# Larger slots and coarser operations in an L2 pooling kernel: three 51.5 KB input slots, stores for two loads each, and small loads at the end

## The chip, the cores and the metric

The kernel runs on one core of a Trainium2 chip. The metric is the time of one execution on the device in microseconds; the median of nine runs stands for a kernel. VectorE is called DVE here and ScalarE ACT, as in the profile; SP is the engine whose queue issues most DMAs.

## The reference

The input x is 32 x 256 x 4096 float32 (134.2 MB), and p is 2. Every four neighbours in the last axis become one output, the root of the mean of their squares; the output is 32 x 256 x 1024 float32 (33.6 MB).

```python
for i in range(length // kernel_size):
    window = np.abs(x[:, :, i * kernel_size:(i + 1) * kernel_size]) ** p
    result[:, :, i] = np.mean(window, axis=-1) ** (1.0 / p)
```

Since windows never cross rows, the whole input can be taken as one flat array, cut into pieces whose length is a multiple of four, with the matching quarter of each piece as output.

## The kernel before

The flat input is 128 partitions times 262144 columns. It is cut into 32 loads of 8192 columns (`W`), 4 MiB each and 32 KB per partition. Four input tiles rotate (`in_pool`, `bufs=4`). The loads are collected into groups: seven groups of four, one of three and one of one. A group is a contiguous block of the input, in which a partition's part is contiguous too; each load takes a stretch of it (`x_block`, L65), and the group's output is stored by one DMA (`out_block`, L70).

The order is written by hand; each engine runs its own instructions in the order of the program, and the waits follow from the data. The SP queue issues the loads (L79): three ahead of the loop, and in round i of the loop load i + 3, which waits until the tile it overwrites has been summed. In round i the load's two halves of 4096 columns (`CH`) are taken in turn:

- ACT squares the half in place (L108).
- DVE sums each four squares into the group's output tile with a reduction (L112).
- ACT takes the root of the half before this one, with the factor 1/4 in its scale (L87), so that it need not wait for the sum of the half just squared. When that ends a group, ACT's queue issues the group's store (L91).

```python
held = {len(groups) - 1 - LAST - j for j in range(2)}
...
        if i == first + g - 1 and c + CH == W and group_of[i] not in held:
            nc.scalar.dma_start(out=out_block(group_of[i]), in_=ot)
...
    root(*pending)
    for gi in sorted(held):
        nc.sync.dma_start(out=out_block(gi), in_=ots[gi])
```

The stores of groups 6 and 7 are held back: they are issued on SP after all loads (L122), so that they lie in the DMA queue behind the last load. Two output tiles rotate among the groups and the last group has its own.

Of the kernel before, what the change touches and what calls it, by code (L numbers as in the profile page):

```python
# [1 line left out]

# [4 lines left out]


@with_exitstack
def kernel(  # L10
    ctx: ExitStack,
    tc: tile.TileContext,
    x: bass.AP,
    p: float,
    kernel_size: int,
    out: bass.AP,
):

    nc = tc.nc

    assert float(p) == 2.0, "kernel specialized for p == 2"
    k = int(kernel_size)
    assert k == 4, "kernel specialized for kernel_size == 4"  # L30

    P = nc.NUM_PARTITIONS
    fp32 = mybir.dt.float32
    xf = x.rearrange("b c l -> (b c l)")
    of = out.rearrange("b c l -> (b c l)")
    total = xf.shape[0] // P

    W = 8192
    CH = 4096
    GROUP = 4  # L40
    LAST = 1
    n = total // W
    assert n * W == total


    groups = []
    i = 0
    while i < n - LAST:
        g = min(GROUP, n - LAST - i)
        groups.append((i, g))  # L50
        i += g
    groups += [(j, 1) for j in range(n - LAST, n)]
    held = {len(groups) - 1 - LAST - j for j in range(2)}
    group_of = {}
    for gi, (first, g) in enumerate(groups):
        for j in range(g):
            group_of[first + j] = gi

    in_pool = ctx.enter_context(tc.tile_pool(name="in_pool", bufs=4))
    out_pool = ctx.enter_context(tc.tile_pool(name="out_pool", bufs=2))  # L60
    last_pool = ctx.enter_context(tc.tile_pool(name="last_pool", bufs=1))
    ctx.enter_context(tc.manual_schedule())


    def x_block(i):  # L65
        first, g = groups[group_of[i]]
        block = xf[first * W * P:(first + g) * W * P].rearrange("(p w) -> p w", p=P)
        return block[:, (i - first) * W:(i - first + 1) * W]

    def out_block(gi):  # L70
        first, g = groups[gi]
        return of[first * W * P // k:(first + g) * W * P // k].rearrange("(p w) -> p w", p=P)

    xts = {}
    ots = {}

    def load(i):
        xt = in_pool.tile([P, W], fp32)
        nc.sync.dma_start(out=xt, in_=x_block(i))  # L79
        xts[i] = xt  # L80

    def root(i, c):
        first, g = groups[group_of[i]]
        ot = ots[group_of[i]]
        at = ((i - first) * W + c) // k
        o = ot[:, at:at + CH // k]
        nc.scalar.activation(  # L87
            out=o, in_=o, func=mybir.ActivationFunctionType.Sqrt, scale=1.0 / k,
        )
        if i == first + g - 1 and c + CH == W and group_of[i] not in held:  # L90
            nc.scalar.dma_start(out=out_block(group_of[i]), in_=ot)  # L91

    for i in range(3):
        load(i)

    pending = None
    for i in range(n):
        if i + 3 < n:
            load(i + 3)
        gi = group_of[i]  # L100
        first, g = groups[gi]
        if i == first:
            pool = last_pool if i >= n - LAST else out_pool
            ot = pool.tile([P, g * W // k], fp32)
            ots[gi] = ot
        for c in range(0, W, CH):
            xh = xts[i][:, c:c + CH]
            nc.scalar.activation(  # L108
                out=xh, in_=xh, func=mybir.ActivationFunctionType.Square,
            )  # L110
            at = ((i - first) * W + c) // k
            nc.vector.tensor_reduce(  # L112
                out=ots[gi][:, at:at + CH // k],
                in_=xh.rearrange("p (n j) -> p n j", j=k),
                axis=mybir.AxisListType.X, op=mybir.AluOpType.add,
            )
            if pending is not None:
                root(*pending)
            pending = (i, c)
    root(*pending)  # L120
    for gi in sorted(held):
        nc.sync.dma_start(out=out_block(gi), in_=ots[gi])  # L122


# [1 line left out]
_INS = ['x', 'p', 'kernel_size']  # L126
_OUTS = [((32, 256, 1024), 'float32')]

_NUMBERS = {'p': 2.0, 'kernel_size': 4}


# [26 lines left out]
```

## Time and profile before

| | |
|---|---|
| median of 9 runs | 395.78 us (395.55 to 395.92) |
| the profiled execution, its own time | 395.87 us |
| its span in the trace | 393.7 us |
| ACT busy | 294.8 us (75%), 130 instructions |
| DVE busy | 282.8 us (72%), 64 instructions |
| HBM read and written | 134.22 MB and 33.55 MB, 426 GB/s over the span |
| DMA packets | 5906 (41 DMAs of 128 rows, 16 completion packets for each, 2 of the instruction queue) |
| load, issue to landing | 35.9 us median, 32 of them, 4096 KB each |

The span runs from the first instruction of the program to the last; the 2.2 us between it and the execution's time lie outside. A load's 35.9 us from issue to landing is mostly waiting in the queue: up to four are in flight. The part of the page on DMA queues divides the traffic in this way (columns: queue, packets, megabytes, and the time that the packets took as a share of sixteen DMA engines over the span):

```profile
q1 hardware_dynamic: 4896, 141.56, 83.9%
q10 hardware_dynamic: 1008, 26.21, 15.5%
q14 instruction: 2, 0.02, 0.0%
```

Queue q1 carries what SP issues: 32 loads and two stores. Queue q10 carries ACT's seven stores. The last one fetches instructions. The shares sum to over 99%.

### The profile page before, as it was taken

What the parts mean: (1) busy time and instruction counts of PE and PEld (TensorE: products, weight loads), DVE (VectorE), ACT (ScalarE), POOL (GpSimd) and SP (SyncE); (2) the same over time, 40 slices, a digit from 0 to 9 for tenths busy, and PEclk for the clock granted to TensorE, in tenths of its full rate; (3) what the DMA queues carried; (4) which work ended last, traced back from release to release, by engine and by line L of the source; (5) the groups of instructions that cost most, each with busy time, mean ns of one, the idle gap of its engine ahead of it and who ended that gap; (6) DMA issues with size and microseconds to landing.
All of it is one profiled execution on the core that took longest, in us unless ns stands there. A gap on an engine that the chain in (4) does not pass through costs nothing.

```text
span 393.7 us, 357 instructions
## 1 busy us (share of the span) xinstructions
DVE 282.8 (72%) x64; ACT 294.8 (75%) x130; POOL 0.2 (0%) x4
## 2 busy tenths in 40 slices
DVE  0399996729976399764988559866598846999992
ACT  1699987469883798828988189863998819999981
POOL 0000000000000000000000000000000000000000
DMA  8999999999999999999999999999999999999997
GB/s 346 453 426 426 426 426 383 436 449 433 430 426 426 426 443 430 450 430 433 426 426 426 436 433 443 437 430 430 426 426 436 436 436 440 430 433 426 426 435 314
DMA packets 5906, 167.79 MB, mean 426 GB/s; under 512 B 656, under 2 KB 656, under 8 KB 656
## 3 DMA queue, kind: packets, MB, share of 16 engines
q1 hardware_dynamic: 4896, 141.56, 83.9%
q10 hardware_dynamic: 1008, 26.21, 15.5%
q14 instruction: 2, 0.02, 0.0%
HBM read 134.22 MB, written 33.55 MB: 426 GB/s over the span
## 4 chain that ended last, share of the span: by engine, by line
DMA 72%; ACT 17%; DVE 9%; SPq 0%; issue 0%; ACTq 0%
DMA xt<-in_x_dram 72%; ACT xt L108 14%; DVE ot L112 9%; ACT ot L87 2%; SPq L79 0%; ACTq L108 0%
## 5 line engine op out<-in xcount | busy, mean ns | idle before, releaser
L112 DVE TENSOR_REDUCE ot<-xt 128x1024 f32<-128x4096 f32 x64 | 282.8, 4420 | 103.3 <-ACT xt L108 102.5
L108 ACT ACTIVATE xt<-xt 128x4096 f32<-128x4096 f32 x64 | 231.0, 3611 | 87.5 <-DMA xt<-in_x_dram 84.9
L87 ACT ACTIVATE ot<-ot 128x1024 f32<-128x1024 f32 x64 | 67.1, 1048 | 4.2 <-DVE ot L112 3.4
L108 ACT ACT_TABLE_LOAD x1 | 1.3, 1283 | 0.7 <-PEq L139 0.7
L87 ACT ACT_TABLE_LOAD x1 | 1.3, 1283 | 0.0
L139 POOL MEMSET const-bfloat16-1.0<- 128x1 bf16 x1 | 0.1, 103 | 0.0
L139 POOL MEMSET const-uint8-127<- 128x1 uint8 x1 | 0.1, 103 | 0.0
L139 POOL MEMSET const-float32-1.0<- 128x1 f32 x1 | 0.1, 100 | 0.0
L139 POOL MEMSET const-float32-0.0<- 128x1 f32 x1 | 0.1, 99 | 0.2 <-issue 0.2
## 6 DMA issues: line engine op xcount, KB each, us to landing
xt<-in_x_dram SPq DMA_DIRECT2D x32, 4096.0 KB, 35.9
out_dram<-ot ACTq DMA_DIRECT2D x6, 4096.0 KB, 23.6
out_dram<-ot SPq DMA_DIRECT2D x1, 4096.0 KB, 34.1
out_dram<-ot SPq DMA_DIRECT2D x1, 3072.0 KB, 12.3
out_dram<-ot ACTq DMA_DIRECT2D x1, 1024.0 KB, 5.6
```

The lines of the kernel that those rows point to most:

```text
L87: nc.scalar.activation(out=o, in_=o, func=mybir.ActivationFunctionType.Sqrt, scale=1.0 / k,)
L108: nc.scalar.activation(out=xh, in_=xh, func=mybir.ActivationFunctionType.Square,)
L112: nc.vector.tensor_reduce(out=ots[gi][:, at:at + CH // k], in_=xh.rearrange("p (n j) -> p n j", j=k), axis=mybir.AxisListType.X, op=mybir. ...
L139: nc = _bacc.Bacc("TRN2", target_bir_lowering=False, num_devices=1)
```

## The change

Three input tiles of 13184 columns (51.5 KB per partition) replace four of 8192, and two output tiles of 6592 columns (25.8 KB) replace the former ones. There are 22 loads instead of 32: loads 0 to 17 fill a slot each, loads 18 and 19 share a slot, and so do 20 and 21 (6592, 6592, 6592 and 5056 columns). Groups 0 to 8 have two loads each, group 9 has loads 18 to 20, and group 10 load 21. There are 11 stores instead of 9.

In loads 0 to 15 one square and one sum take the whole load. Loads 16 and 17 are taken in halves of 6592, load 21 in halves of 2528. One root of 6592 columns is taken per group in groups 0 to 8, and it stands on ACT behind the square of the following piece (`LAG`). At the end roots are finer: one for loads 18 and 19 together, one for load 20, and one for each half of load 21.

From load 17 on (`PAIRS`), the sum is made by two tensor additions in place of one reduction: neighbours are added in place at every second column, and then columns 0 and 2 of every four are added into the output.

The stores of groups 7 to 10 (`late`) are issued on SP, in order, after all loads. The outputs of groups 9 and 10 have no output tile: they lie in the third input tile, which load 17 was the last to use (`in_x`).

```diff
-    W = 8192
-    CH = 4096
-    GROUP = 4
-    LAST = 1
...
+    W, O_W = 13184, 6592
+    X_SLOTS, O_SLOTS = 3, 2
+    slots = [[(W, [W])]] * 16 + [[(W, [6592, 6592])]] * 2
+    slots += [[(6592, [6592]), (6592, [6592])], [(6592, [6592]), (5056, [2528, 2528])]]
+    groups = [2] * 9 + [3, 1]
+    late = {7, 8, 9, 10}
+    in_x = {9: (2, 0), 10: (2, 4944)}
+    FINE, ENDS, LAG = {21}, {19, 20}, 1
+    PAIRS = 17
...
+    def root(g, o, ends):
+        nc.scalar.activation(out=o, in_=o, func=Act.Sqrt, scale=1.0 / k)
+        if ends and g not in late:
+            store(g, nc.scalar)
...
+    def total_sum(o, v, i):
+        add = mybir.AluOpType.add
+        if i < PAIRS:
+            nc.vector.tensor_reduce(
+                out=o, in_=v.rearrange("p (n j) -> p n j", j=k),
+                axis=mybir.AxisListType.X, op=add,
+            )
+            return
+        h = v.rearrange("p (m t) -> p m t", t=2)
+        nc.vector.tensor_tensor(out=h[:, :, 0], in0=h[:, :, 0], in1=h[:, :, 1], op=add)
+        q = v.rearrange("p (n j) -> p n j", j=k)
+        nc.vector.tensor_tensor(out=o, in0=q[:, :, 0], in1=q[:, :, 2], op=add)
...
+        while ahead < n and loads[ahead][0] < s + X_SLOTS:
+            load(ahead)
+            ahead += 1
...
+        for step in chunks:
+            v = xs[i][:, c:c + step]
+            nc.scalar.activation(out=v, in_=v, func=Act.Square)
+            total_sum(ots[g][:, summed:summed + step // k], v, i)
+            while pending and pending[0][0] <= done - LAG:
+                root(*pending.pop(0)[1:])
...
+            ends = summed == columns[g] // k
+            if ends or i in FINE or (i in ENDS and c == w):
+                pending.append((done - 1, g, ots[g][:, rooted:summed], ends))
+                rooted = summed
+    for job in pending:
+        root(*job[1:])
+    for g in sorted(late):
+        store(g, nc.sync)
```

More of the change, by code (lines that the diff above doesn't have):

```diff
@@ L33 @@
     fp32 = mybir.dt.float32
+    Act = mybir.ActivationFunctionType
     xf = x.rearrange("b c l -> (b c l)")
@@ L36 @@
     total = xf.shape[0] // P
-    W = 8192
-    CH = 4096
-    GROUP = 4
-    LAST = 1
[L42 to L57, printed above, removed]
@@ L59 @@
-    in_pool = ctx.enter_context(tc.tile_pool(name="in_pool", bufs=4))
-    out_pool = ctx.enter_context(tc.tile_pool(name="out_pool", bufs=2))
-    last_pool = ctx.enter_context(tc.tile_pool(name="last_pool", bufs=1))
-    ctx.enter_context(tc.manual_schedule())
[L65 to L72, printed above, removed]
@@ L74 @@
-    xts = {}
-    ots = {}
[L77 to L91, printed above, removed]
@@ L93 @@
-    for i in range(3):
-        load(i)
-    pending = None
-    for i in range(n):
[L98 to L119, printed above, removed]
@@ L120 @@
-    root(*pending)
-    for gi in sorted(held):
-        nc.sync.dma_start(out=out_block(gi), in_=ots[gi])
+    W, O_W = 13184, 6592
[7 more added lines that the diff above has]
+    PAIRS = 17
+    loads = [(s, sum(w for w, _ in slot[:j]), *slot[j]) for s, slot in enumerate(slots)
+             for j in range(len(slot))]
@@ new lines @@
+    n = len(loads)
+    assert sum(w for _, _, w, _ in loads) == total
+    firsts = [sum(groups[:g]) for g in range(len(groups))]
+    assert sum(groups) == n
+    group_of = [g for g, count in enumerate(groups) for _ in range(count)]
+    columns = [sum(w for _, _, w, _ in loads[firsts[g]:firsts[g] + groups[g]])
+               for g in range(len(groups))]
+    x_pool = ctx.enter_context(tc.tile_pool(name="x_pool", bufs=1))
+    o_pool = ctx.enter_context(tc.tile_pool(name="o_pool", bufs=1))
@@ new lines, with block, load @@
+    x_tiles = [x_pool.tile([P, W], fp32, name=f"xt{j}") for j in range(X_SLOTS)]
+    o_tiles = [o_pool.tile([P, O_W], fp32, name=f"ot{j}") for j in range(O_SLOTS)]
+    ctx.enter_context(tc.manual_schedule())
+    def block(flat, g, div):
+        at, width = sum(columns[:g]) * P // div, columns[g] * P // div
+        return flat[at:at + width].rearrange("(p w) -> p w", p=P)
+    xs = {}
+    def load(i):
+        s, at, w, _ = loads[i]
+        v = x_tiles[s % X_SLOTS][:, at:at + w]
+        g = group_of[i]
+        src = sum(loads[j][2] for j in range(firsts[g], i))
+        nc.sync.dma_start(out=v, in_=block(xf, g, 1)[:, src:src + w])
+        xs[i] = v
@@ new lines, with store @@
+    ots = {}
+    def store(g, queue):
+        queue.dma_start(out=block(of, g, k), in_=ots[g])
+    def root(g, o, ends):
[14 more added lines that the diff above has]
+        nc.vector.tensor_tensor(out=o, in0=q[:, :, 0], in1=q[:, :, 2], op=add)
@@ new lines @@
+    ahead = 0
+    while ahead < n and loads[ahead][0] < X_SLOTS - 1:
+        load(ahead)
+        ahead += 1
+    pending = []
+    done = 0
+    for i in range(n):
+        s, _, w, chunks = loads[i]
+        while ahead < n and loads[ahead][0] < s + X_SLOTS:
+            load(ahead)
+            ahead += 1
+        g = group_of[i]
+        if i == firsts[g]:
+            t, first = (o_tiles[g % O_SLOTS], 0) if g not in in_x else (x_tiles[in_x[g][0]], in_x[g][1])
+            ots[g] = t[:, first:first + columns[g] // k]
+            summed = rooted = 0
+        assert sum(chunks) == w
+        c = 0
+        for step in chunks:
[4 more added lines that the diff above has]
+                root(*pending.pop(0)[1:])
+            done += 1
+            c += step
+            summed += step // k
+            ends = summed == columns[g] // k
+            if ends or i in FINE or (i in ENDS and c == w):
+                pending.append((done - 1, g, ots[g][:, rooted:summed], ends))
+                rooted = summed
```

## The prediction

> **What bounds the kernel now.** I read the page's slices first (part 2), because they show whether one resource is full all the way through.
>
> ```profile
> DVE  0399996729976399764988559866598846999992
> ACT  1699987469883798828988189863998819999981
> ...
> DMA  8999999999999999999999999999999999999997
> GB/s 346 453 426 426 426 426 383 436 449 433 430 426 426 426 443 430 450 430 433 426 426 426 436 433 443 437 430 430 426 426 436 436 436 440 430 433 426 426 435 314
> ```
>
> The 16 DMA engines are at nine tenths or more in every slice but the first and the last; DVE and ACT have holes everywhere. The table by stages says how full the middle is (columns: stretch, its length, busy time and count of DVE, ACT and POOL, clock, DMA share, GB/s):
>
> ```profile
> 60.00:350.00 290.00, 209.62 (x48) 216.77 (x97) 0.00 (x0) 1.00 1.00 432
> 350.00:380.00 30.00, 27.38 (x7) 28.25 (x13) 0.00 (x0) 1.00 1.00 433
> 380.00:390.00 10.00, 6.10 (x2) 3.79 (x3) 0.00 (x0) 1.00 0.97 407
> 390.00:394.00 4.00, 0.00 (x0) 0.00 (x0) 0.00 (x0) 1.00 0.40 170
> ```
>
> DMA share 1.00 at 432 GB/s up to 380 us. So only three things can change the time: DMA work itself, the dead time at both ends, and any hole that appears in the DMA stream. Next, the rows of part 5 give the prices:
>
> ```profile
> L112 DVE TENSOR_REDUCE ot<-xt 128x1024 f32<-128x4096 f32 x64 | 282.8, 4420 | 103.3 <-ACT xt L108 102.5
> L108 ACT ACTIVATE xt<-xt 128x4096 f32<-128x4096 f32 x64 | 231.0, 3611 | 87.5 <-DMA xt<-in_x_dram 84.9
> L87 ACT ACTIVATE ot<-ot 128x1024 f32<-128x1024 f32 x64 | 67.1, 1048 | 4.2 <-DVE ot L112 3.4
> ```
>
> The two ACT rows give 0.834 ns a column and 194 ns fixed. Last, the end of the timeline shows why there is no hole now: the held stores are issued while earlier transfers still run.
>
> ```profile
> 373.61 3.62 ACT L108 ACTIVATE xt<-xt 128x4096 f32<-128x4096 f32 x1 [0.55 <-DMA xt<-in_x_dram]
> ...
> 378.20 0.34 SPq L122 DMA_DIRECT2D out_dram<-ot  x1
> ...
> 387.25 0.34 ACTq L91 DMA_DIRECT2D out_dram<-ot  x1
> ```
>
> The last load lands at 373.5. The store of group 6 (4 MiB, 9.7 us) covers 373 to 382, group 7's (issued at 378.2) covers 382 to 390, and the last, issued at 387.25, follows without a gap.
>
> [...]
>
> **DMA work.** The bytes stay. Before, 32 loads and 9 stores have 128 rows each, 8 per engine: 328 packets an engine. After, 22 loads and 11 stores: 264. The trace's packet records have 32 KB in 1213 ns, 24 KB in 912, 8 KB in 309: 36.8 ns per KB and 8 ns over, of which 4 overlap the next packet. 64 x 4 ns = 0.3 us gained. Bounds 0 and 0.6 (no overlap).
>
> **Instruction fetches.** Part 3 of the page has two packets on the instruction queue; they stand at 159.7 and 250.8 us in the packet records, and the DMA engine beside them finishes at 392.5, the other fifteen between 391.5 and 392.0. As the built programs list them, ACT's instructions shrink from 137 to 47 and DVE's from 66 to 34, so I take these fetches as gone: 0.5 us, bounds 0 and 0.6. The start (first packet at 1.74 us) and the slow first store (its neighbours took about 1.2 us longer at 58 us) stay: first load and first ACT-queue store are there as before, counted at nothing.
>
> **Steady part.** A square of 13184 columns is 0.19 + 13184 x 0.834 ns = 11.2 us, a sum 13.9 (14.2 if all 4420 ns scale), a root of 6592 is 5.7. Loads land 9.71 us apart for 4 MiB when alone (22.47, 32.18, 41.90), so a 13184-column load takes 15.6 us, 23.4 beside a store of 7.8. Per two loads ACT has 28.1 us and DVE 27.8 against 39.0 of DMA: no bound. Refill of three slots, at its tightest: load 0 lands at about 18.8, is squared at 30.0 and summed at 43.9, so load 3's packets start at 44.9 (1 us from issue to first packet, as at 0.73 to 1.74), while loads 0 to 2 keep the queue full until 48.5. Slot 1 is 3.6 us early likewise (60.5 against 64.1). From load 4 on, a store widens this. The new wait of a sum for the store two groups before it is met about 6 us early (root and issue 18 us after a load's landing, 23.4 for the transfer, against 51 us); behind it only DVE's next sums queue. The sums that the SP loads wait for are the same waits as now, with longer sums. Cost 0; a lost cover would cost 1 us per us of lateness, not more.
>
> **The end.** Here the cover is thin. Stores 7 to 10 (three groups and the last load) go out on SP behind all loads, in order (before, two on SP and the last on ACT's queue); store 9 needs the root of load 20, and store 10 is queued behind its wait; nothing else is. Count from T, the landing of load 16. DMA still has load 17 (15.6), loads 18 to 20 (7.8 each), load 21 (6.0), stores 7 and 8 (7.8 each) and about 1 us of store 6: it runs dry at T - 0.4 + 61.6 = T+61.2. Without a penalty the engines go: ACT squares 16a, roots group 7, squares 16b, 17a, 17b, 18 (5.6 us each: 5.69 less 0.09 overlap) until T+33.7. DVE sums 16a by reduce (7.0) to 12.8, 16b, which waits for its square, from 16.9 to 24.0. Then come pairs of additions: 3296 outputs[...] and 1648 (1.87 us), 5.46 a pair. 17a and 17b end at 34.9, root of group 8 at 40.6, squares 19 and 20 at 46.2 and 51.8, sum 19 at 51.7, the joint root of 18 and 19 (2.9) at 54.7, square 21a at 56.9, sum 20 at 57.2, its root (1.6) at 58.8: store 9's first packet at T+59.8, 1.4 us early. So with the plain price nothing is lost.
>
> But the second addition reads every fourth fp32, a step of 16 bytes[...]. The first steps 8 bytes[...] and is priced plainly. For the second I bound the price from 1 cycle an element (1.87 us[...]) to 2 cycles[...]. I take 2, an estimate[...]. A pair is then 7.2 us. 17a and 17b end at 38.4; root of group 8 at 44.1; pair 18 at 45.6; squares 19, 20 at 49.7, 55.3; pair 19 at 56.9; the joint root at 59.8; square 21a 62.0; pair 20 at 64.1; its root 65.7; first packet 66.7. DMA stands still from 61.2 to 66.7: 5.5 us. Store 9 (5.9 us) then lasts to 72.6, and store 10, ready at about 71.6 + 1, follows. A further 0.1 us for each of the two to three dependent pairs on this path makes it 5.7.
>
> **Sum.** The profiled execution took 395.87 us (span 393.7 and 2.2 around it), 0.09 over the median. 395.87 - 0.3 - 0.5 + 5.7 = 400.8; against the median, 400.7.
>
> **Rivals.** *The second addition costs its plain price* (chance 0.41). [...] Then store 9 is in time and 395.78 - 0.8 = 395.0, or 395.1 with a little of the 1.4 us margin lost; not slower. It decides at about 1.25 cycles an element, where the margin is used up. [...]second addition 2.73 us, pair 6.3; the path grows by four times 0.86, 3.4, less the margin of 1.4, and the same 0.1: +2.1, 397.1 (0.12). *A refill hole*: slots 0 or 1 come free over 3.6 us late, because sums of 13184 take more than the 14.2 us above; each us late is added once or twice, 396 to 398 with the plain price (0.03). That the change does nothing at all is excluded: the instructions do differ.
>
> **Numbers.** Forecast (2 cycles) 400.7, own range 399.8 to 402.2, chance 0.44. A measurement of this kernel tells about 0.2% (0.8 us) from no change. Slower: 0.44 + 0.12 + 0.01 of the refill case = 0.57. The plain-price case, centred at 395.1, splits near 395.0: 0.18 faster and 0.23 same, to which the refill case adds 0.02: 0.25. Range: from 394.7 to 401.6, leaving out about 0.08 below and 0.1 above.
>
> **What would show it.** Right: additions of 1648 outputs near 3.6 us, DMA share near zero for 5 to 6 us just before the last two stores, the last but one store issued after its predecessor has landed. Packets about 4750 (33 x 144), fewer instruction fetches. Wrong: 1.87 us for that row and an unbroken DMA line; or a DMA dip near 48 or 64 us, which would be the refill.

## The result, and the profile after

The changed kernel takes 398.07 us (median, 397.31 to 398.54); the kernel before, over all its runs beside it, 395.70 us. The ratio is 1.0058 (95% interval 1.005 to 1.0067): slower by 2.4 us. The forecast was 400.7 us, slower by 5.0. The profiled execution took 398.41 us with a span of 396.4, against 395.87 and 393.7.

First the slices of the changed kernel's page (tenths of a slice, 9.9 us each):

```profile
DVE  0009898695959296929691969296919697699594
ACT  1095699929880998199619962996299639997973
...
DMA  8999999999999999999999999998999999999967
GB/s 341 426 458 442 431 436 436 359 434 474 397 466 436 426 426 418 426 434 436 458 452 426 391 455 428 428 468 386 434 436 439 476 426 426 394 436 428 435 287 321
```

The DMA row stands at nine tenths, with a single 8, up to the last slice but one, where it drops to 6 and 287 GB/s; before, it fell only in the last. The table by stages puts a place to it (stretch, its length, busy time and count of DVE, ACT, POOL, clock, DMA share, GB/s):

```profile
60.00:300.00 240.00, 170.29 (x13) 174.46 (x21) 0.00 (x0) 1.00 1.00 432
...
350.00:380.00 30.00, 25.22 (x9) 25.77 (x6) 0.00 (x0) 1.00 1.00 428
380.00:383.00 3.00, 2.97 (x2) 3.00 (x2) 0.00 (x0) 1.00 0.98 422
383.00:385.00 2.00, 2.00 (x2) 0.67 (x1) 0.00 (x0) 1.00 0.16 66
385.00:388.00 3.00, 2.78 (x3) 2.88 (x2) 0.00 (x0) 1.00 0.25 105
388.00:392.00 4.00, 2.75 (x2) 1.77 (x3) 0.00 (x0) 1.00 0.93 396
```

From 60 to 300 us the DMA is as full, at the same 432 GB/s, as before. Between 383 and 388 us it nearly stands still, while DVE has no idle time in the first two of these microseconds and 0.2 us in the next three: now DVE is what is waited for. The chain that ended last shows this less well than it seems to: DMA has fallen from 72% of the span to 47%, and DVE has risen from 9% to 22%. But 14 of these 22 are the reductions (L93), nearly all of them in the stretch where the DMA is full, and the first experiment below, which has no hole, shows 47% and 19%. So the hole is read from the table by stages and from the timeline, not from these shares (before; the change, by engine and by line; the first experiment):

```profile
DMA 72%; ACT 17%; DVE 9%; SPq 0%; issue 0%; ACTq 0%
...
DMA 47%; ACT 24%; DVE 22%; issue 6%; SPq 0%; ACTq 0%
DMA xt<-in_x_dram 47%; ACT xt L123 18%; DVE ot L93 14%; ACT ot L86 6%; DVE xt L99 4%; DVE xt L101 2%; DVE ot L101 2%; ACT xt L86 1%; ACT L86 0%; SPq L77 0%; ACTq L83 0%
...
DMA 47%; ACT 26%; DVE 19%; issue 6%; SPq 0%; ACTq 0%
```

What DVE does there, and at what price, is in the groups kept apart by shape (line, engine, operation, output and input, count, busy us, mean ns of one, idle before):

```profile
L93 DVE TENSOR_REDUCE ot<-xt 128x3296 f32<-128x13184 f32 x16 | 222.2, 13886 | 105.2 <-ACT xt L123 105.2
L123 ACT ACTIVATE xt<-xt 128x13184 f32<-128x13184 f32 x16 | 179.1, 11191 | 91.9 <-DMA xt<-in_x_dram 90.2 <-ACT ot L86 1.7
L86 ACT ACTIVATE ot<-ot 128x6592 f32<-128x6592 f32 x9 | 51.2, 5685 | 2.9 <-DVE ot L101 2.9
...
L99 DVE TENSOR_TENSOR xt<-xt 128x3296 f32<-128x3296 f32 x5 | 18.0, 3595 | 4.6 <-ACT xt L123 4.6
...
L101 DVE TENSOR_TENSOR xt<-xt 128x1648 f32<-128x1648 f32 x3 | 9.4, 3148 | 0.1
```

L101 is the second addition. It has half as many outputs as the first (L99), and yet takes 3.15 us against 3.60: 1.7 times the 1.87 us that the prediction calls its plain price. The trace of before has no addition, so the forecast's prices were its author's estimates: 3.59 us for a first one of 3296 outputs (3.60 here) and 1.87 to 3.59 for a second one; the 1.87 is measured below. The end of the timeline shows where that lands (start, us, engine, line, in brackets the idle time before it and what ended it):

```profile
323.07 5.70 ACT L123 ACTIVATE xt<-xt 128x6592 f32<-128x6592 f32 x1 [9.56 <-DMA xt<-in_x_dram]
...
360.34 5.70 ACT L86 ACTIVATE ot<-ot 128x6592 f32<-128x6592 f32 x1 [2.93 <-DVE ot L101]
...
381.96 3.13 DVE L101 TENSOR_TENSOR xt<-xt 128x1648 f32<-128x1648 f32 x1
...
385.12 1.58 ACT L86 ACTIVATE xt<-xt 128x1648 f32<-128x1648 f32 x1 [1.45 <-DVE xt L101]
...
386.73 6.12 SPq L83 DMA_DIRECT2D out_dram<-xt  x2
```

T is 323.07: taken here and below as the start of load 16's square, some 0.4 us after the load has landed. The root of group 8 and the root of load 20 both wait for a second addition, and store 9 goes out at 386.73, T+63.7. The packet records hold, for each DMA, sixteen completion packets (528 for 33 DMAs), taken here as one from each DMA engine; in what follows "the middle one" is the median of the sixteen and "the latest one" the last, and a hole is the time from there to the next DMA's first packets. Store 8 ends at 383.4 us on the middle one of the sixteen DMA engines and at 385.2 on the latest; store 9's first packets stand at 387.6. The hole is 4.3 us on most engines, and 2.4 on the latest one. The latest one sets the end: the span before and its hole make 393.7 + 2.4 = 396.1, against the span of 396.4.

### The profile page after: what moved, and what is told of

Read it like the earlier page. It is cut to its first block, busy times and chain, and to the rows that moved or that the text cites. A ratio compares the mean times of both kernels' runs of the same rounds, so it can differ in the third digit from the quotient of the medians.

```text
span 396.4 us, 192 instructions
## 1 busy us (share of the span) xinstructions
DVE 274.9 (69%) x32; ACT 281.7 (71%) x40; POOL 0.2 (0%) x4
## 2 busy tenths in 40 slices
DMA packets 4752, 167.77 MB, mean 423 GB/s; under 512 B 528, under 2 KB 528, under 8 KB 656
## 4 chain that ended last, share of the span: by engine, by line
DMA 47%; ACT 24%; DVE 22%; issue 6%; SPq 0%; ACTq 0%
DMA xt<-in_x_dram 47%; ACT xt L123 18%; DVE ot L93 14%; ACT ot L86 6%; DVE xt L99 4%; DVE xt L101 2%; DVE ot L101 2%; ACT xt L86 1%; ACT L86 0%; SPq L77 0%; ACTq L83 0%
## 5 line engine op out<-in xcount | busy, mean ns | idle before, releaser
L93 DVE TENSOR_REDUCE ot<-xt 128x3296 f32<-128x13184 f32 (+1 forms) x18 | 236.2, 13123 | 110.8 <-ACT xt L123 108.9
L123 ACT ACTIVATE xt<-xt 128x13184 f32<-128x13184 f32 (+2 forms) x25 | 223.2, 8938 | 102.1 <-DMA xt<-in_x_dram 100.4
L86 ACT ACTIVATE ot<-ot 128x6592 f32<-128x6592 f32 x9 | 51.2, 5685 | 2.9 <-DVE ot L101 2.9
L99 DVE TENSOR_TENSOR xt<-xt 128x3296 f32<-128x3296 f32 (+1 forms) x7 | 20.9, 2991 | 5.8 <-ACT xt L123 5.8
L101 DVE TENSOR_TENSOR xt<-xt 128x1648 f32<-128x1648 f32 (+1 forms) x5 | 12.0, 2404 | 0.2
L86 ACT ACTIVATE xt<-xt 128x632 f32<-128x632 f32 (+2 forms) x4 | 6.0, 1493 | 5.0 <-DVE xt L101 5.0
L101 DVE TENSOR_TENSOR ot<-xt 128x1648 f32<-128x1648 f32 x2 | 6.2, 3125 | 0.1
```

The costliest lines, as they stand in the source:

```text
L86: nc.scalar.activation(out=o, in_=o, func=Act.Sqrt, scale=1.0 / k)
L93: nc.vector.tensor_reduce(out=o, in_=v.rearrange("p (n j) -> p n j", j=k), axis=mybir.AxisListType.X, op=add,)
L99: nc.vector.tensor_tensor(out=h[:, :, 0], in0=h[:, :, 0], in1=h[:, :, 1], op=add)
L101: nc.vector.tensor_tensor(out=o, in0=q[:, :, 0], in1=q[:, :, 2], op=add)
L123: nc.scalar.activation(out=v, in_=v, func=Act.Square)
```

## The experiments

The theory is that the price of the second addition, whose inputs step 16 bytes, makes store 9 late. The rivals are other parts of the change: the coarse operations, the store layout, the transfers themselves. Beside each run the kernel before was timed on the same chip; it took 395.6 to 395.8 us there. What is read from packet records is always that of one profiled execution.

**The second addition reads every second column.** The first addition writes its sums side by side, so that the second steps 8 bytes; the number of outputs is the same.

```diff
-        nc.vector.tensor_tensor(out=h[:, :, 0], in0=h[:, :, 0], in1=h[:, :, 1], op=add)
-        q = v.rearrange("p (n j) -> p n j", j=k)
-        nc.vector.tensor_tensor(out=o, in0=q[:, :, 0], in1=q[:, :, 2], op=add)
+        m = v.shape[1] // 2
+        nc.vector.tensor_tensor(out=v[:, :m], in0=h[:, :, 0], in1=h[:, :, 1], op=add)
+        q = v[:, :m].rearrange("p (n j) -> p n j", j=2)
+        nc.vector.tensor_tensor(out=o, in0=q[:, :, 0], in1=q[:, :, 1], op=add)
```

> The first addition of a pair writes its results side by side, so that the second reads every second column (8 bytes apart) instead of columns 0 and 2 of four (16 bytes apart); nothing else changes. Theory (the 16-byte step makes the second addition slow, and DVE's queue is what store 9 waits for): the second addition of 1648 outputs falls from 3.13 us to about 1.87, a pair from 6.73 to 5.46, store 9 is issued about 5 us earlier relative to the landing of load 16, before store 8 has left the queue; the hole of 2.4 us on the latest DMA engine goes, and the time is 395.4 to 395.8, a ratio of 0.999 to 1.000. Rival (the small loads and ACT's own work at the end make the hole): still 397 to 398. Rival (the larger slots make the steady part slower): still above 397 with no hole at the end.

Measured: 395.71 us, ratio 1.0004 (0.9995 to 1.0012). Its group of second additions, its table by stages and the issue of store 9:

```profile
L102 DVE TENSOR_TENSOR xt<-xt 128x1648 f32<-128x1648 f32 x3 | 5.6, 1874 | 0.1
```

```profile
380.00:383.00 3.00, 1.92 (x2) 3.00 (x2) 0.00 (x0) 1.00 0.98 422
383.00:386.00 3.00, 2.29 (x2) 1.23 (x3) 0.00 (x0) 1.00 0.99 426
```

```profile
381.36 5.66 SPq L83 DMA_DIRECT2D out_dram<-xt  x2
```

The addition takes 1.87 us, the plain price of the prediction, store 9 goes out at T+58.8 (T is 322.53), the very time that the prediction worked out for the plain price, and the hole is gone. One access pattern is worth the whole 2.4 us.

**The duration alone, put back.** To the kernel above, two additions in a scratch tile are added between the two additions of each pair of loads 17 to 20. Their results are not used; they add only to DVE's time.

```diff
+    scratch = o_pool.tile([P, 450], fp32, name="scratch")
+    nc.vector.memset(scratch, 0.0)
...
+        if m > 2000:
+            for _ in range(2):
+                nc.vector.tensor_tensor(out=scratch, in0=scratch, in1=scratch, op=add)
```

> The kernel with the 8-byte step, and between the two additions of each pair of loads 17 to 20 DVE also adds a scratch tile of 450 columns to itself twice (2 x 0.63 us, results unused), which puts back the 1.25 us by which the 16-byte step was slower. Theory (the time comes from DVE's duration alone): the hole before store 9 is back, 2 to 2.5 us on the latest DMA engine, and the time is that of the changed kernel, 397.7 to 398.4. Rival (the 16-byte step did harm in another way, or the layout of the sums matters): about 395.7.

Measured: 397.47 us, ratio 1.0052 (1.0038 to 1.0065). The two groups:

```profile
L105 DVE TENSOR_TENSOR scratch<-scratch 128x450 f32<-128x450 f32 x10 | 6.2, 624 | 0.2
L107 DVE TENSOR_TENSOR xt<-xt 128x1648 f32<-128x1648 f32 x3 | 5.6, 1869 | 0.0
```

The loss comes back with time that touches none of the kernel's data: store 9 goes out at 385.66, T+62.9, and the hole on the latest engine is about 1.7 us. The median is 0.2 us under the expected range, since operations overlap a little (a second addition starts at 375.67 us, 0.08 before the two in the scratch tile end): from start to start, a pair on the path is 1.03 us longer here than in the first experiment, and 1.21 longer in the change. Over four pairs that is 0.7 us, by which store 9 goes out sooner than in the change. So it is DVE's duration that counts, not something else that the access pattern might do.

**One reduction in place of the additions.** `PAIRS = 99` in place of 17.

> The sums of loads 17 to 21 are made by one reduction each, as for the other loads, in place of two additions. Theory: a reduction of 6592 columns takes 7.02 us against 6.73 for the pair; four of them lie on the path to store 9, so the hole grows by about 1.2 us, and the time is 399.0 to 399.5 (ratio 1.009). So the pair as written saves only 1 us or so of the 6 us that a pair at the plain price would save (4 times 7.02 - 5.46). Rival (ACT sets the end): no change, 398.

Measured: 399.31 us, ratio 1.0092 (1.0078 to 1.0106), inside the expectation. Store 9 goes out at T+64.7, and the hole on the latest engine is 3.4 us, 1.0 longer than in the change:

```profile
383.00:386.00 3.00, 3.00 (x1) 1.35 (x1) 0.00 (x0) 1.00 0.08 35
```

A reduction of 6592 columns takes 7.0 us, a pair 6.7. The pairs of the change are thus a little better than what they replace, but only with the closer step (5.5 us) are they fast enough.

**Store 9 in two parts.** Loads 18 and 19 are stored apart from load 20.

```diff
-        store(g, nc.sync)
+        if g == 9:
+            cut = 3296
+            nc.sync.dma_start(out=block(of, g, k)[:, :cut], in_=ots[g][:, :cut])
+            nc.sync.dma_start(out=block(of, g, k)[:, cut:], in_=ots[g][:, cut:])
+        else:
+            store(g, nc.sync)
```

> The store of group 9 is cut in two: the outputs of loads 18 and 19 go out as soon as their joint root is done, those of load 20 after its own root; sums as in the changed kernel (16-byte step). Theory (DVE's chain sets when the last results exist, not how they are stored): the hole before store 9 closes, since its first part is issued 5 us earlier, but a hole of about 2.4 us opens before store 10, whose results still come 69.4 us after the landing of load 16; no gain, 397.8 to 398.3. Rival (the fault is that store 9 is one large piece waiting for its last part): the 2.4 us are won, 395.7.

Measured: 398.07 us, ratio 1.0063 (1.005 to 1.0076), as slow as the change. The issues, and the stage in which the hole now lies:

```profile
381.22 0.33 SPq L139 DMA_DIRECT2D out_dram<-xt  x1
386.45 0.33 SPq L140 DMA_DIRECT2D out_dram<-xt  x1
392.23 0.33 SPq L83 DMA_DIRECT2D out_dram<-xt  x1
```

```profile
390.00:392.00 2.00, 1.40 (x2) 0.53 (x1) 0.00 (x0) 1.00 0.05 20
```

The hole moves behind the split parts, in front of store 10: what is late is the end of the work of ACT and DVE, whatever is stored in between.

**Coarse operations undone, in loads 0 to 15.** `[[(W, [W])]] * 16` becomes `[[(W, [6592, 6592])]] * 16`: halves, as before the change.

> Loads 0 to 15 are squared and summed in halves of 6592 again (one root per store stays). Theory (the loss lies in the tail alone; the steady part has 3.6 us and more of cover at each refill): no change beyond 0.5 us, 397.6 to 398.5. Rival (coarse operations delay refills or stores in the middle): 0.5 to 2 us faster.

Measured: 399.00 us, ratio 1.0084 (1.007 to 1.0098): not as expected, 0.9 us slower than the change. Store 9 is issued at T+63.6 as in the change, but T is 323.96, 0.9 later. Two instruction fetches stood at 295.3 and 351.1 us, so two explanations were left: the fetches (theory B), or that finer operations issue store 6 sooner, so that its packets pass ahead of load 16's last ones (theory A). The next run tells them apart.

**Halves in loads 12 to 15 alone**, with the rest as in the change.

> Only loads 12 to 15 are taken in halves. Taking all of 0 to 15 in halves cost 0.9 us where I had expected nothing. Theory A: with halves the root of group 6 comes after half a square, so that store 6 starts some 5.6 us earlier and gets ahead of load 16; load 16 lands 0.9 us later and less of store 6 is left as cover after it: then these four loads do all of it, 399.0, and load 16 lands near 324.0 us. Theory B: the longer program fetches instructions in mid-run (at 295 and 351 us) and one DMA engine falls behind: then, with fewer added instructions and no fetch before load 16, 398.1.

Measured: 400.46 us, ratio 1.012 (1.0106 to 1.0134). No fetch stood ahead of the end, and yet it is slower still, so theory B doesn't account for it. T is 325.11, 2.0 us later than in the change, and store 9 follows at T+63.6 again:

```profile
388.75 6.12 SPq L83 DMA_DIRECT2D out_dram<-xt  x2
```

In the packet records, store 6 lands 6.0 us after load 16 in the change (328.7 and 322.7), 0.6 us ahead of it with halves everywhere (322.9 and 323.5), and 0.1 ahead of it here (324.6 and 324.7). Its last packets then no longer lie behind T, and the latest engine runs dry at T+60.2 in both runs, against T+62.1 in the change. That is theory A in kind: store 6 is issued at 296.13 us with halves everywhere and at 297.50 here, at 301.93 in the change, and both runs lose the same 1.9 us of cover. That the loss comes out as 0.9 us in the one run and 2.4 in the other, 1.5 more than expected, goes with how late the latest DMA engine is: it ends store 8 at 384.2 us with halves everywhere (0.7 behind the middle one), at 385.2 in the change (1.8 behind) and at 385.3 here (2.1 behind). Why it differs from run to run wasn't found.

**The price by itself.** A kernel that only times operations on tiles: three of each, 1648 outputs, with one thing changed at a time. A few of its lines:

```python
        nc.vector.tensor_tensor(**tt(flat, at(xt, 2), at(yt, 2)))
        nc.vector.tensor_tensor(**tt(flat, at(xt, 3), at(yt, 3)))
        nc.vector.tensor_tensor(**tt(flat, at(xt, 4), at(yt, 4)))
        nc.vector.tensor_tensor(**tt(at(ot, 4), x1, y1))
```

> No pooling at all: three tiles are loaded and fp32 additions of 1648 outputs run one after the other on DVE with various steps of their inputs and outputs, then squares on ACT; the output is one tile. Theory (the step of 16 bytes on the reading side is the cost): inputs with steps of 1 and 2 columns take 1.87 us, of 4 about 3.1, of 8 about the same; with one of the two inputs at step 4 also near 3.1; the pattern of the kernel (columns 0 and 2 of the same tile) 3.1. Rival (it is two readings of the same line from both inputs that collide): separate tiles at step 4 take 1.87 and only the pattern of the kernel 3.1. Rival (a step of the output or in-place writing costs): additions with a stepped output are slower and those with stepped inputs are not.

Measured (L60, L62, L64, L66 are additions with both inputs at steps 2, 3, 4 and 8; L74 has step 4 on the output alone; L81, L83, L85 are ACT squares with steps 1, 2 and 4):

```profile
L85 ACT ACTIVATE ot<-yt 128x1648 f32<-128x1648 f32 x3 | 9.4, 3144 | 0.1
L66 DVE TENSOR_TENSOR ot<-xt,yt 128x1648 f32<-128x1648 f32 x3 | 9.3, 3113 | 0.1
L74 DVE TENSOR_TENSOR ot<-xt,yt 128x1648 f32<-128x1648 f32 x3 | 9.2, 3079 | 0.1
...
L64 DVE TENSOR_TENSOR ot<-xt,yt 128x1648 f32<-128x1648 f32 x3 | 9.2, 3075 | 0.1
...
L62 DVE TENSOR_TENSOR ot<-xt,yt 128x1648 f32<-128x1648 f32 x3 | 7.1, 2364 | 0.1
...
L60 DVE TENSOR_TENSOR ot<-xt,yt 128x1648 f32<-128x1648 f32 x3 | 5.6, 1875 | 0.1
L83 ACT ACTIVATE ot<-yt 128x1648 f32<-128x1648 f32 x3 | 5.3, 1770 | 0.1
L81 ACT ACTIVATE ot<-yt 128x1648 f32<-128x1648 f32 x3 | 4.7, 1577 | 0.1
```

The cost is flat up to step 2 (1875 ns), rises at step 3 (2364), is full at step 4 (3075) and hardly higher at 8 (3113). It is the same with one input (3078 ns), both (3075), or the output at step 4 (3079), and with the kernel's own pattern, columns 0 and 2 of one tile (3072); so it is neither two inputs meeting in one line, since separate tiles pay it too, nor the output alone. DVE's fixed time follows from two plain additions: 3595 ns for 3296 outputs (L99) and 1875 for 1648 make 1.04 ns an element and 155 ns over. Without these, step 4 costs (3075 - 155)/1648 = 1.77 ns an element, step 3 (2364 - 155)/1648 = 1.34, three quarters of it. These prices suggest a count: with a tile divided into lines of 16 bytes, a division of the author's that no trace shows, four elements at step 3 touch three lines, at step 4 four lines, at step 2 only two.

**Does the count of lines give every pattern?** If so, a cost of about 1.78 ns for each line touched (at step 4 above, DVE 1.77 and ACT 1.79), with the engine's own rate as the least, should do so.

```python
        nc.vector.tensor_tensor(**tt(flat, at(xt, 5), at(yt, 5)))
        nc.vector.tensor_tensor(**tt(out2, rows(xt, 8, 2), rows(yt, 8, 2)))
        nc.vector.tensor_tensor(**tt(at(ot, 4), at(xt, 4), at(yt, 4)))
        nc.scalar.activation(out=sq, in_=at(yt, 3), func=Act.Square)
```

> No pooling: loads three tiles, then fp32 additions of 1648 outputs and squares with other steps; one tile is stored. Theory ([...]an element costs the larger of the engine's own rate and its share of lines): additions at step 5 and 7 take 3.07 to 3.12 us as at 4; at step 3 2.36; pairs of neighbours out of every four (two elements a line) 1.88; pairs out of every eight also 1.88; inputs and output all at step 4 3.1, not double; squares on ACT at step 3 near 2.4 us, at step 5 3.14, with the output at step 4 3.14. Rival (the cost grows with the distance, or adds up over operands): steps 5 and 7 above 3.2, and all three at step 4 well above 3.1.

Measured (L72 has all three operands at step 4; L64 is step 5; L70 takes two neighbours out of every eight; L75 is ACT at step 3):

```profile
L64 DVE TENSOR_TENSOR ot<-xt,yt 128x1648 f32<-128x1648 f32 x3 | 9.5, 3157 | 0.1
L72 DVE TENSOR_TENSOR ot<-xt,yt 128x1648 f32<-128x1648 f32 x3 | 9.4, 3147 | 0.1
...
L75 ACT ACTIVATE ot<-yt 128x1648 f32<-128x1648 f32 x3 | 7.3, 2418 | 0.1
...
L70 DVE TENSOR_TENSOR ot<-xt,yt 128x1648 f32<-128x1648 f32 x3 | 5.6, 1875 | 0.1
```

Two neighbours out of eight step 32 bytes from pair to pair and still cost the plain price (1875 ns), as the count of two elements to a line has it. Three strided operands cost hardly more than one (3147 ns against 3078). A price by the size of the step is refuted (3113 ns at step 8, 3075 at step 4); one by lines touched fits all patterns within 3%, but for ACT at step 2 (1770 ns; half a line an element gives 200 + 1648 x 0.89 = 1667). The 200 ns are ACT's fixed time, 1577 - 1648 x 0.834 with the prediction's price of a column. That the price goes by lines is a rule that fits the durations, not something seen in a trace.

**The gain that didn't come.** Without the hole the change should be 0.8 us faster than before, by the prediction's first two steps; the first experiment is not (395.71). In its packet records the middle DMA engine ends at 390.8 us, before at 391.7: 1.0 earlier. But the latest one ends at 392.2, 1.4 behind the middle one; before, 392.5, 0.7 behind. (The thirteen executions of the first experiment lie between 394.93 and 396.42 us, so the lag may well change from one to the next.) Two runs look for the lag's cause, both on top of the first experiment's edit. The one puts the steady stores on SP's queue:

```diff
-            store(g, nc.scalar)
+            store(g, nc.sync)
```

> The kernel with the 8-byte step, and the stores of groups 0 to 6 issued on SP's queue, where they stand between the loads, in place of ACT's. The 8-byte kernel gained nothing on the kernel before though its middle DMA engine ends 1 us earlier, because the latest engine lags the middle one by 1.4 us (0.9 in the kernel before). Theory (engines drift apart where packets of 51 KB and 26 KB from two queues alternate): with one queue the lag shrinks to below 1 us, and the time to 394.9 to 395.3. Rival (the lag comes from the start and from stalls that strike a few engines whatever the queue): 395.5 to 396.

Measured: 397.13 us, ratio 1.004 (1.0026 to 1.0054): refuted. The spread between the first and the last DMA engine grows from 1.3 us to 1.9, 2.4, 2.7 and 3.1 as stores start, and the latest engine ends at 393.7, the middle one at 391.1. Two queues are not the cause of the lag; with one it is larger.

The other cuts each full load in two DMAs of 25.8 KB per partition:

```diff
+        if w == W:
+            cut = w // 2
+            nc.sync.dma_start(out=v[:, :cut], in_=block(xf, g, 1)[:, src:src + cut])
+            nc.sync.dma_start(out=v[:, cut:], in_=block(xf, g, 1)[:, src + cut:src + w])
+        else:
+            nc.sync.dma_start(out=v, in_=block(xf, g, 1)[:, src:src + w])
```

> The kernel with the 8-byte step, and each load of 13184 columns made of two DMAs of 6592. Theory (drift comes from large packets): the lag between engines shrinks, 395.2 to 395.5 in spite of 144 more packets per engine at 4 ns each (0.6 us). Rival (packet size does not matter to the lag): 0.3 to 0.6 us slower than the 8-byte kernel, 396.0 to 396.3.

Measured: 395.82 us, ratio 1.0004 (0.9995 to 1.0012). The lag falls to 0.7 us, but the middle engine ends at 391.6, 0.8 later, with 18 times 8 more packets an engine. Two instruction fetches also stand near the end again (351.7 and 381.2 us), which the first experiment doesn't have. Each theory is half right, and the time stays.

**Fewer fetches alone.** The kernel before with whole-load squares, sums and roots, but halves for the last two loads:

```diff
+    def step(i):
+        return W if i < n - 2 else CH
...
-        for c in range(0, W, CH):
-            xh = xts[i][:, c:c + CH]
+        for c in range(0, W, step(i)):
+            xh = xts[i][:, c:c + step(i)]
...
```

> The kernel before with one square, one sum and one root per load of 8192 columns in loads 0 to 29; DMAs, tiles and the last two loads as they were. Theory (my prediction's term: its long instruction list makes fetches in mid-run that set one DMA engine back, and a shorter list saves 0.5 us): no fetch in mid-run, latest engine within 0.5 us of the middle one, 395.0 to 395.3 (ratio 0.9985 to 0.999). Rival (another engine lags in its place, or the fetch costs nothing): 395.6 to 395.8, or slower where coarser operations lengthen the end.

Measured: 395.89 us, ratio 1.0007 (0.9999 to 1.0015). Inconclusive: whole loads close to the end delayed the last store from 387.25 to 389.73 us, and a hole opened in front of it, 1.6 us on the middle DMA engine and 0.8 on the latest; one fetch was left, at 260.6 us. The same edit with `n - 6` leaves the end alone:

> The kernel before with whole-load squares, sums and roots for loads 0 to 25 and halves for the last six, so that its end is as in the kernel before (last store issued near 387.3 us, DMA share 0.97 from 380 to 390 us) with some 50 to 60 fewer instructions on ACT. If fewer instruction fetches shorten the time by 0.3 to 0.5 us, as the prediction's step has it: 395.1 to 395.4. If they are worth nothing because the DMA engine that is held up is not the one that sets the end: 395.5 to 395.8, with the DMA engine that ends last still near 392.5.

Measured: 395.14 us, ratio 0.999 (0.9981 to 0.9998). Its stage at the end and its row for fetches:

```profile
380.00:390.00 10.00, 5.37 (x2) 3.07 (x3) 0.00 (x0) 1.00 0.99 419
```

```profile
q14 instruction: 1, 0.01, 0.0%
```

One fetch of the two is gone, and 0.5 us with it. In the packet records the latest engine ends at 391.75 instead of 392.47, and it is 0.4 behind the middle one instead of 0.7. So of 0.7 us in the trace some 0.3 is lag of one engine, as fewer fetches would have it, and 0.4 is common to all engines, whose cause was not traced further. This is the fastest of the kernels, by 0.1%. Its interval just leaves out no change, that of the first experiment does not.

## Why the prediction was right in direction and too large

1. *What bounds the kernel, and the steady part at nothing*: right. The share is 1.00 at 432 GB/s from 60 to 300 us. The square took 11.19 us (11.2 said), the sum 13.89 (13.9, an estimate), the root 5.69 (5.7). Load 3 was issued at 44.1 us (sum due at 43.9), and no dip stands near 48 or 64 us.
2. *The end runs out of cover, because each second addition delays store 9*: right, shown by taking the stride away (no hole, -2.4 us) and by putting only the duration back (+1.8 us).
3. *"I take 2, an estimate"*: the step that failed, the price of the second addition. The second addition was taken at 3.59 us; it took 3.13 to 3.15. The "cycle" of the prediction is the plain price of an element, measured at 1.04 ns (with 155 ns over, from L99 and the plain 1875 ns); 3.59 us is two of these an element, and 3.13 to 3.15 is 1.73 to 1.74. Four pairs on the path, 6.7 instead of 7.2 us each, bring store 9 to T+63.7 instead of T+65.7: 2.0 us too much. It was put between two bounds and taken at the upper one, an estimate that no run of before backed; the rival midway between the bounds, 2.73 us, likewise an estimate, gave 397.1, and the result lies between the two. (The plain case's margin of 1.4 us is used up by four pairs at 1.2 plain prices an element, 1648 x 1.04 x 0.2 ns more each, not at the 1.25 that the rivals give.)
4. *"About 1 us of store 6"* behind T: 1.9 us were left, as long as two of its packets take (978 ns each). The latest engine ran dry at T+62.1, not T+61.2: 0.9 us too much. That this term depends on when store 6 starts, and not on bytes, is what the runs with halves showed: it can be 0.
5. With these, 5.5 - 2.0 - 0.9 and 0.1 less from issue to first packet give 2.5 us, against 2.4 measured on the latest engine. The added 0.2 us for dependent pairs wasn't seen.
6. *0.3 for packets and 0.5 for fetches*: there on the middle DMA engine (1.0 us in the first experiment), but not in the time, which the latest engine sets. The step added up work for each DMA engine and took all sixteen as equal, which they are not (1.4 us from the middle one to the latest in the first experiment). The packets (4752) and the missing fetch row were right: the page lists two queues only,

```profile
q1 hardware_dynamic: 3744, 144.15, 84.6%
q10 hardware_dynamic: 1008, 23.63, 13.8%
```

The terms as measured: 395.87 + 0 + 2.4 = 398.3 us, against the profiled 398.41. The forecast for that execution was 400.8. That it was 2.4 us too high and not 3.2 is luck: the gain of 0.8 us that didn't come hides a part of what the end was overpriced.

## What to carry to other kernels

When a transfer-bound kernel is changed, write down for its end the time at which the transfers run dry and the time at which the last results are ready, with every operation of the chain at a price measured for its access pattern: a difference of 1.3 us in one small addition, four times in a row, decided here. For strided fp32 operands, count the 16-byte lines that they touch, a count that fits these durations, as well as their elements: at 1648 outputs DVE took 1875 ns at step 2 and 3075 at step 4. Writing the intermediate sums side by side cost nothing (3.59 us for the first addition, 3.60 in the change) and keeps two elements to a line. And take a gain in transfer work as real only if the slowest DMA engine gets it: in the first experiment the middle one ended 1.0 us earlier, the latest 0.3, and the time stayed at 395.71 us.

## What the runs showed of the hardware that was not expected

- Strided fp32 operands cost DVE and ACT alike: the times fit about 1.78 ns for each 16-byte line that an operand touches (DVE at step 4: 1.77; ACT: (3144 - 200)/1648 = 1.79), with their own 1.04 and 0.83 ns an element as the least. Inputs and outputs count alike (DVE: 3075 and 3079 ns at step 4; ACT: 3144 and 3100), and three strided operands cost hardly more than one (3147 against 3078 ns). With two elements to a line DVE pays nothing more (1875 ns at step 2, as at step 1), ACT a little (1770 ns against 1577). The line is a count that fits; no trace shows it.
- The sixteen DMA engines drift apart: the latest ended 1.4 to 2.1 us behind the middle one in the changed kernel and most of its variants, 2.6 with stores and loads on one queue, 0.7 with loads cut in two DMAs, but 0.7 also with whole loads and halved operations. With one queue it grew in jumps where stores stand. The size of the packets alone doesn't account for it, and why some engines are held up stays open.
- Issuing store 6 some 4 to 6 us sooner, in a part where the DMA is full either way, took 1.9 us of cover at the end (0.9 and 2.4 us of time in the two runs with halves): it passed ahead of load 16's last packets, so the chain that starts with load 16 started later.
